# Later places for the sums of squared attention outputs and for the query transposes in a hand-ordered attention

## The chip, the cores and the metric

The kernel runs on one core of a Trainium2 chip. The metric is the device time of one execution in microseconds (us), the median of several runs. The engines are named as in the profile: PE is TensorE, DVE is VectorE, ACT is ScalarE, POOL is GpSimd and SP is SyncE, which here only issues DMAs.

## The reference

The reference is a backbone of two layers over 512 latent tokens and 256 context tokens of width 1024. Layer 0 mixes tokens by differential attention, layer 1 by a short gated convolution, and each ends with a SwiGLU FFN; adaLN shifts, scales and gates come from a conditioning vector. The part that matters here is the attention of layer 0, with 8 heads of two maps of 64 and a value width of 128:

```python
def _diff_attend(q, k, v, lam):
    s = jnp.einsum("bqmhd,bkmhd->bmhqk", q, k) * (HEAD_DIM ** -0.5)
    p = jax.nn.softmax(s, axis=-1)
    a = (p[:, 0] - lam * p[:, 1]).astype(v.dtype)
    return jnp.einsum("bhqk,bkhd->bqhd", a, v)

q = rmsnorm(q, q_norm); k = rmsnorm(k, k_norm)        # per head and map
q_l, k_l = apply_rope(q_l, cos, sin), apply_rope(k_l, cos, sin)
o = rmsnorm(o, subln) * (1.0 - lam_init)              # per token and head
y = o.reshape(bsz, -1, DIFF_V_WIDTH) @ w_o
```

Queries are the 512 latent tokens, keys and values all 768. The last norm needs, for each token and head, the sum of the squares of the attention's 128 outputs.

## The kernel before, in words

Activations lie with features on partitions. Every float32 product is made of three products of fp32r parts (high by high, high by low, low by high), so each operand is split into two parts: ACT casts the high part, DVE or POOL subtracts the low one.

The attention is a pipeline over the heads. While head h is attended, the projections of head h+1 are made token tile by token tile (`pq_{h+1}_t`, 24 products of 384 columns, or of 256 for the context tiles 4 and 5), and during head 7 the output projection of the first six heads (`pw_n`). A head takes 24 positions, each with a quarter of such a tile. What else is issued stands in an agenda that `events` (L635 to L644) fills from tables of positions (L15 to L38): `trans_k` (tiles `tk_h_g`: transposes of two token tiles of keys; ACT casts KH, DVE subtracts KL), `trans_q` (tile `tq_h`; ACT casts Q0 and Q1, DVE subtracts), `scores` (tiles `s_h_t_m`, the row maximum `l` on DVE, the exponentials `e` on ACT), `trans_a` (tiles `ta_h_t_g`: transposes of the attention weights; ACT casts ATh, DVE subtracts ATl) and `pv` (tile `pv_h_half`: attention weights times values for half of the queries, 18 products of 256 columns). All these PSUM tiles except the scores and projections come from one pool, `ptr`, with tag "tr" and 2 buffers: a tile's first write waits until the tile two before it has been read by ACT and DVE.

At the end of `pv` ACT squares the outputs into `osq` (L539) and copies them to `oT` (L540), DVE takes the minimum with a bound (L541), TensorE sums the squares with two small float32 products into a tile `po_h_half` (L542 to L545) and DVE adds that tile to `stat` (L546). In head 6 `o_rstd` (L553) turns the sums of the first six heads into `or_0`; SP stores it to `rst_dram` (L562) and loads it back, broadcast to all partitions, into `obc0` to `obc5` (L567); DVE scales the outputs `oT` with it (L568); they are split into the parts `oh` and `ol` for `pw_n`. The tiles `h_n` (L624) hold the residual stream and lie over `aTh_n`, an operand of the projections. `ada` (L191) are DVE products of streamed adaLN weights that fill the attention, with a raw buffer that the `obc` and the output weights `raw_wo` share.

In the start TensorE is pinned to the order of the program; from L366 on it is not, and a list scheduler orders the instructions of every engine from the order of issue and its own estimates. TensorE, DVE, ACT, POOL and SP each run their queue in that order.

Of the kernel before, what the change touches and what calls it, by code (L numbers as in the profile page):

```python
# [7 lines left out]
F32 = mybir.dt.float32  # L8
# [6 lines left out]
# The order of issue in the attention. A head takes 24 positions, each with a quarter of the projections of  # L15
# one token tile of the next head (head 7: of one feature tile of the output projection); what else is issued,
# and at which position of its head, is listed here.
#   scores 0, scores 1, transpose 0, scores 2, transpose 1, scores 3, transpose 2, P V of tiles 0-1, transpose 3, P V of tiles 2-3
AT = (6, 9, 11, 12, 16, 16, 20, 19, 22, 28)
AT_OF = {0: (10, 14, 16, 16, 20, 21, 22, 21, 26, 27), 1: (7, 8, 11, 12, 12, 16, 21, 19, 23, 28),  # L20
         6: (8, 9, 14, 6, 16, 17, 23, 18, 24, 28), 7: (5, 7, 10, 9, 13, 8, 16, 15, 16, 23)}
#   transposes of k tiles 2-3, q, k tiles 4-5 (head 0: k tiles 0-1, 2-3, q, k tiles 4-5)
TK = (2, 0, 4)
TK_OF = {0: (9, 9, 8, 10), 1: (0, 2, 4), 7: (3, 0, 3)}
#   transposes of k tiles 0-1 of the next head
TK_NEXT = 16
TK_NEXT_OF = {0: 12, 6: 15}
#   the weights of the head after the next, by feature tiles
W_AT = (16, 19, 22, 23, 23, 24, 26, 27)
W_AT_OF = {0: (11, 11, 15, 22, 22, 22, 25, 26)}  # L30
#   positions from the squares of a token tile to its rotation
LAG = 1
LAG_OF = {1: 0}
#   head 6: scale of the first six heads' outputs, its products, their exact parts
# [3 lines left out]
# halves of adaLN tiles per token tile of each head, per pair of gate and up tiles, per down tile  # L38
ADA_HEAD = (0, 2, 1, 1, 1, 1, 1, 1)
ADA_GATE, ADA_DOWN = 3, 3  # L40
# tile of the output projection before which the weights of the last two heads are staged
W67_AT = 6
# token tiles whose squares the activation engine also sums
ACC_TILES = (0, 1, 2, 3, 4)
# second parts of staged weights: 0 on the vector engine, 1 on the GpSimd engine
# [6 lines left out]
# the first head's projections: at which feature tile the second head's weights are staged, how many tiles the  # L52
# context lags behind the latent tokens, where its statistics and their broadcast come
# [5 lines left out]
# pieces of the second half of the tokens after which the next norm's statistics and its products come  # L59
TURN = {8: (4, 7), 2: (1, 3)}  # L60
# feature tiles whose squares GpSimd sums for the norm after the attention
POOL_SUMS = (1, 3, 5)
P = 128
# [3 lines left out]
KT = 8  # L67
# [10 lines left out]
# columns of the packed parameters  # L78
# [9 lines left out]
class InOrder:  # L88
    """an engine; while pin is set its instructions are issued in program order"""
# [16 lines left out]
def kernel(  # L106
# [43 lines left out]
    mods = const.tile([P, 2, 6, KT], F32, name="mods")      # sh1 sc1 g1 sh2 sc2 g2  # L150
    part = const.tile([P, 2, 2, 6, KT], F32, name="part")   # halves of the dot products
    mod0 = const.tile([P, 2, 2, KT], F32, name="mod0")      # layer 0, latent and context: sh1 sc1
    Gc = const.tile([P, 5, KT], F32, name="Gc")             # norm gains times (1 + scale)
# [9 lines left out]
    # staging of the attention weights and the attention output: right stack  # L163
# [22 lines left out]
    def ada_half(i, half, pool, tag, bufs):  # L186
        """one half of the dot products of a tile of 128 columns of ada_w with silu(c)"""
# [15 lines left out]
    # =====================================================================  # L203
    # layer 0: modulated input, differential attention
    # =====================================================================
# [23 lines left out]
    # the tensor engine's clock rises while the first loads are under way  # L229
# [25 lines left out]
    def bcast(dgs, bc):  # L255
        """bc[t][:, q] = rstd of token q of tile t, the same on all partitions"""
        for dg, o in zip(dgs, bc):
            te.matmul(out=o, lhsT=ones, rhs=dg, start=True, stop=True)
# [827 lines left out]
```

## Time and profile before

| | |
|---|---|
| median of 3 runs | 1342.76 us (1341.63 to 1345.31) |
| profiled execution, span from first to last instruction | 1343.2 us |
| mean granted TensorE clock | 0.991 |
| PE busy | 1309.2 us (97%) |
| DVE busy | 809.6 us (60%) |
| ACT busy | 503.9 us (38%) |
| POOL busy | 184.9 us (14%) |
| attention (heads 0 to 7) | from about 66 to 399 us, some 40 us a head |

The shares of the whole span say little on the attention: DVE's 60% is an average over the attention and the FFNs, where it has little to do. The windows of a stretch show what each engine does in it; the list of waits shows for which producer TensorE sat idle; the timelines show single instructions, with the idle time before each and what ended it in brackets.

### The profile page before, as it was taken

The page shows a single profiled execution, that of the slowest core. Times are in us where ns is not written, and L with a number is a line of the kernel's source. Part 1 is how long each engine was busy: PE and PEld are TensorE (multiplying, and loading weights), DVE is VectorE, ACT ScalarE, POOL GpSimd, SP SyncE. Part 2 cuts the span into 40 slices and gives each one's busy share as a digit, 9 for nine tenths or more (in the row PEclk, how much of TensorE's full clock was granted, in tenths as well). Part 3 has the DMA queues.
Part 4 walks back from the last instruction along what each step waited for, and adds up shares of the span by engine and source line. Part 5 has one row for each costly group of instructions (what it writes and reads, how often), then busy time and mean ns, then how long its engine had stood idle before and what let it go on. Part 6 is the DMA issues. An engine that isn't in the chain of part 4 may idle for free.

```text
span 1343.2 us, 18899 instructions
## 1 busy us (share of the span) xinstructions
PE 1309.2 (97%) x7021; PEld 1130.8 (84%) x7021; DVE 809.6 (60%) x1598; ACT 503.9 (38%) x1125; POOL 184.9 (14%) x239
## 2 busy tenths in 40 slices
PE   8999999999999999899999999999999999999999
PEld 7889988998789888688888898888898888888887
DVE  5889888988968666665653366444664333333331
ACT  4677666776655321122221333222342212222120
POOL 0544444543302000000000020000100000000000
PEclk9999999999998999899999999999999999999999
DMA  9413333214333756677642333313323223322231
GB/s 350 160 41 112 94 95 90 71 59 146 106 118 103 224 197 196 198 241 224 203 134 67 110 109 109 97 55 96 118 72 121 81 72 109 125 94 85 70 105 40
DMA packets 72284, 164.59 MB, mean 123 GB/s; under 512 B 7784, under 2 KB 23424, under 8 KB 71168
## 3 DMA queue, kind: packets, MB, share of 16 engines
q1 hardware_dynamic: 72192, 163.38, 38.6%
q8 instruction: 55, 0.90, 0.3%
q14 instruction: 37, 0.30, 0.1%
HBM read 161.24 MB, written 2.11 MB: 122 GB/s over the span
## 4 chain that ended last, share of the span: by engine, by line
PE 74%; DVE 10%; DMA 8%; issue 3%; POOL 2%; ACT 2%; SPq 0%; POOLq 0%; DVEq 0%; ACTq 0%
PE pg L98 25%; PE pd L98 18%; PE pi L98 8%; PE pq L98 7%; DMA ada<-in_adaR_dram 6%; PE py L98 3%; PE s L98 3%; PE pw L98 3%; DVE ada L191 2%; PE pf_in L98 2%; PE pf_gu L98 2%; PE pv L98 1%; DMA xk<-in_xT_dram 1%; POOL st L432 1%; DMA raw_w<-in_wqkv_dram 1%
## 5 line engine op out<-in xcount | busy, mean ns | idle before, releaser
L727 ACT CAST sh_gu<-sr_gu 128x1024 fp32r<-128x1024 f32 x88 | 92.3, 1052 | 276.1 <-PE pg L98 147.9
L191 DVE SCALAR_TENSOR_TENSOR ada<-ada,scrow 128x512 f32<-128x512 f32 x160 | 110.6, 702 | 85.5 <-DMA ada<-in_adaR_dram 85.1
L728 DVE TENSOR_TENSOR sl_gu<-sr_gu,sh_gu 128x1024 fp32r<-128x1024 f32 x85 | 105.8, 1247 | 72.4 <-ACT sh_gu L727 65.3
L98 PE MATMUL pg<-xl_n0b,sh_gu 128*128 128x512 f32 x320 | 124.6, 389 | 0.0
L98 PE MATMUL pg<-xh_n0b,sh_gu 128*128 128x512 f32 x320 | 124.6, 389 | 0.0
L98 PE MATMUL pg<-xh_n1b,sh_gu 128*128 128x512 f32 x320 | 124.6, 389 | 0.0
L98 PE MATMUL pg<-xl_n1b,sh_gu 128*128 128x512 f32 x320 | 124.5, 389 | 0.0
L98 PE MATMUL pg<-xh_n1b,sl_gu 128*128 128x512 f32 x320 | 124.5, 389 | 0.0
L98 PE MATMUL pg<-xh_n0b,sl_gu 128*128 128x512 f32 x320 | 124.5, 389 | 0.0
L98 PE MATMUL pq<-hi_w,aTl 128*128 128x384 f32 (+1 forms) x336 | 108.5, 323 | 0.0
L98 PE MATMUL pq<-hi_w,aTh 128*128 128x384 f32 x224 | 77.3, 345 | 2.5 <-DVE qn L443 2.5
L839 DVE TENSOR_TENSOR sl<-sl,pg 128x512 f32<-128x512 f32 x40 | 27.4, 686 | 85.7 <-PE pg L98 85.7
L98 PE MATMUL pq<-lo_w,aTh 128*128 128x384 f32 x224 | 76.3, 341 | 0.0
L98 PEld LDWEIGHTS pg<-xh_n1b,sh_gu 128*128 128x128 f32 x320 | 60.1, 188 | 12.5
L98 PEld LDWEIGHTS pg<-xl_n0b,sh_gu 128*128 128x128 f32 x320 | 60.1, 188 | 12.5
L98 PEld LDWEIGHTS pg<-xh_n1b,sl_gu 128*128 128x128 f32 x320 | 60.1, 188 | 12.5
L98 PEld LDWEIGHTS pg<-xh_n0b,sh_gu 128*128 128x128 f32 x320 | 60.1, 188 | 12.5
L98 PEld LDWEIGHTS pg<-xl_n1b,sh_gu 128*128 128x128 f32 x320 | 60.1, 188 | 12.3
L98 PEld LDWEIGHTS pg<-xh_n0b,sl_gu 128*128 128x128 f32 x320 | 60.1, 188 | 12.3
L504 ACT ACTIVATE e<-s,l 128x768 f32<-128x768 f32 x64 | 58.0, 908 | 29.5 <-DVE l L502 18.4
L502 DVE TENSOR_REDUCE l<-s 128x1 f32<-128x768 f32 x64 | 60.0, 949 | 8.3 <-PE s L98 7.8
L98 PEld LDWEIGHTS pq<-hi_w,aTl 128*128 128x128 f32 x336 | 63.9, 190 | 0.0
(390 smaller groups left out, 3366.7 us busy)
## 6 DMA issues: line engine op xcount, KB each, us to landing
sr_gu<-in_wgu_dram SPq DMA_DIRECT2D x88, 512.0 KB, 3.9
ada<-in_adaR_dram SPq DMA_DIRECT2D x160, 256.0 KB, 3.2
raw_w<-in_wqkv_dram SPq DMA_DIRECT2D x64, 192.0 KB, 2.6
sr_in<-in_win_dram SPq DMA_DIRECT2D x24, 512.0 KB, 3.5
ad<-in_ada_dram SPq DMA_DIRECT2D x8, 1024.0 KB, 8.8
raw_wo<-in_wo_dram SPq DMA_DIRECT2D x16, 192.0 KB, 2.8
xk<-in_xT_dram SPq DMA_DIRECT2D x8, 256.0 KB, 5.3
h<-in_xT_dram SPq DMA_DIRECT2D x8, 256.0 KB, 6.1
```

The lines of the kernel that those rows point to most:

```text
L98: ins = f(*args, **kw)
L191: ve.scalar_tensor_tensor(out=raw, in0=raw, scalar=1.0, in1=scrow[:, half * 512:(half + 1) * 512], op0=ALU.mult, op1=ALU.mult, accum_out=p ...
L432: nc.gpsimd.tensor_tensor(out=st[:, 4:4 + ns], in0=st[:, 0:ns], in1=nhalf[:, 0:ns], op=ALU.pow)
L502: ve.tensor_reduce(out=l[:, m:m + 1], in_=s[:, :, 0:384], axis=AX.XY, op=ALU.max, negate=True)
L504: ae.activation(out=em.rearrange("p (a b) -> p a b", a=2), in_=s[:, :, 0:384], func=AF.Exp, bias=l[:, m:m + 1], scale=1.0, accum_out=l[:, ...
L727: ae.copy(out=hi[:, :ncols], in_=raw[:, :ncols])
L728: lo_eng.tensor_tensor(out=lo[:, :ncols], in0=raw[:, :ncols], in1=fp(hi)[:, :ncols], op=ALU.subtract)
L839: ve.tensor_tensor(out=t[:, s], in0=t[:, s], in1=ps_u, op=ALU.mult)
```

## The change

The last part of `pv` becomes a piece of its own, `po`, with its own positions (`PO`): at positions 22 and 35 of a head in most heads, that is, the second half is issued 11 positions into the next head. Before, they came at the positions of `pv`, 19 and 28. The table `TK` moves the query transposes of heads 2 to 6 from position 0 to 2, and those of head 7 from 0 to 3, behind the transposes of key tiles 2 and 3. Comments were taken out as well, which shifts line numbers by some lines.

```diff
+PO = (22, 35)
+PO_OF = {0: (26, 31), 1: (23, 35), 5: (22, 32), 6: (24, 36), 7: (18, 25)}
-TK = (2, 0, 4)
-TK_OF = {0: (9, 9, 8, 10), 1: (0, 2, 4), 7: (3, 0, 3)}
+TK = (2, 2, 4)
+TK_OF = {0: (9, 9, 8, 10), 1: (0, 2, 4), 7: (3, 3, 3)}
...
         ae.activation(out=osq, in_=p, func=AF.Square)
         ae.copy(out=oT[h][:, sl], in_=p)
         ve.tensor_scalar(out=osq, in0=osq, scalar1=BIG, scalar2=None, op0=ALU.min)
+        o.osq[half] = osq
+
+    def po(o, half):
+        h, osq = o.h, o.osq[half]
         p2 = ptr.tile([P, P], F32, name=f"po_{h}_{half}", tag="tr")
         r = slice(64 * half, 64 * half + 64)
         for g in range(2):
...
-        e += zip(AT_OF.get(h, AT), todo)
+        at = AT_OF.get(h, AT)
+        e += zip(at, todo)
+        e += zip(PO_OF.get(h, PO), (lambda: po(o, 0), lambda: po(o, 1)))
```

Since the scheduler starts from another order of issue, the queues of all engines change. Names below end in a running number of the tile.

**TensorE, from head 3 to head 4** (the projections `pq_5` run between). The start of `pq_5_0`, before and then with the change:

```order
L98 MATMUL pq_5_0_2992<-hi_w5_0_2794,aTh0_97 128x384
L98 MATMUL pq_5_0_2992<-lo_w5_0_2795,aTh0_97 128x384
L98 MATMUL pq_5_0_2992<-hi_w5_0_2794,aTl0_113 128x384
L98 MATMUL tq_4_2983<-cst_sb_62,qrp_4_2544 128x128 x4
L98 MATMUL pq_5_0_2992<-hi_w5_1_2861,aTh1_98 128x384
L98 MATMUL pq_5_0_2992<-lo_w5_1_2862,aTh1_98 128x384
```

```order
L101 MATMUL pq_5_0_2983<-hi_w5_0_2794,aTh0_97 128x384
L101 MATMUL pq_5_0_2983<-lo_w5_0_2795,aTh0_97 128x384
L101 MATMUL po_3_0_2922<-osq_3_0_2851,cst_sb_62 32x128 x2
L101 MATMUL pq_5_0_2983<-hi_w5_0_2794,aTl0_113 128x384
L101 MATMUL pq_5_0_2983<-hi_w5_1_2857,aTh1_98 128x384
L101 MATMUL pq_5_0_2983<-lo_w5_1_2858,aTh1_98 128x384
```

`po_3_0` stands now where `tq_4` stood, one product earlier; `tq_4` comes nine products later, right behind `tk_4_1`. The end of `pv_3_1`, before and then with the change:

```order
L98 MATMUL pv_3_1_3049<-ATh_3_1_2882,vl_3_1886 128x256
L98 MATMUL pq_5_1_3093<-hi_w5_0_2794,aTh0_97 128x384
L98 MATMUL pq_5_1_3093<-lo_w5_0_2795,aTh0_97 128x384
L98 MATMUL pq_5_1_3093<-hi_w5_0_2794,aTl0_113 128x384
L98 MATMUL pq_5_1_3093<-hi_w5_1_2861,aTh1_98 128x384
L98 MATMUL pq_5_1_3093<-lo_w5_1_2862,aTh1_98 128x384
L98 MATMUL pq_5_1_3093<-hi_w5_1_2861,aTl1_114 128x384
L98 MATMUL pq_5_1_3093<-hi_w5_2_2928,aTh2_99 128x384
L98 MATMUL po_3_1_3072<-osq_3_1_3068,cst_sb_62 32x128 x2
L98 MATMUL tk_4_2_3076<-cst_sb_62,krp_4_2_2898 128x128 x4
L98 MATMUL pq_5_1_3093<-lo_w5_2_2929,aTh2_99 128x384
```

```order
L101 MATMUL pv_3_1_3049<-ATl_3_1_2879,vh_3_1885 128x256
L101 MATMUL pv_3_1_3049<-ATh_3_1_2878,vl_3_1886 128x256
L101 MATMUL tk_4_2_3072<-cst_sb_62,krp_4_2_2894 128x128 x4
L101 MATMUL pq_5_1_3089<-hi_w5_0_2794,aTh0_97 128x384
L101 MATMUL pq_5_1_3089<-lo_w5_0_2795,aTh0_97 128x384
L101 MATMUL pq_5_1_3089<-hi_w5_0_2794,aTl0_113 128x384
```

`po_3_1` has left (it now stands in `pq_5_2`, in front of `ta_4_0_0`), and `tk_4_2` follows `pv_3_1` at once.

**VectorE, the same stretch**, before and then with the change (from Q0 of head 4 to the min on `osq_3_1`):

```order
L477 TENSOR_TENSOR Q0_4_2425<-tq_4_2983,Q0_4_2425 64x512
L443 TENSOR_TENSOR qn_4_5_2979<-pq_4_5_2901,st_4_5_2958 128x128
L181 TENSOR_TENSOR lo_w5_7_3027<-raw_w5_7_3024,hi_w5_7_3026 128x384
L477 TENSOR_TENSOR Q1_4_2426<-tq_4_2983,Q1_4_2426 64x512
L488 TENSOR_TENSOR KL_4_2428<-tk_4_1_3011,KH_4_2427 128x2x256
L191 SCALAR_TENSOR_TENSOR ada_12_0_3046,part_69<-ada_12_0_3046,scrow_72 128x512
L191 SCALAR_TENSOR_TENSOR ada_12_1_3149,part_69<-ada_12_1_3149,scrow_72 128x512
L191 SCALAR_TENSOR_TENSOR ada_13_0_3230,part_69<-ada_13_0_3230,scrow_72 128x512
L191 SCALAR_TENSOR_TENSOR ada_13_1_3298,part_69<-ada_13_1_3298,scrow_72 128x512
L433 TENSOR_TENSOR vl_5_2972<-pq_5_0_2992,vh_5_2971 128x128
L443 TENSOR_TENSOR qn_5_0_3083<-pq_5_0_2992,st_5_0_3037 128x256
L541 TENSOR_SCALAR osq_3_1_3068<-osq_3_1_3068 128x256
```

```order
L184 TENSOR_TENSOR lo_w5_7_3027<-raw_w5_7_3024,hi_w5_7_3026 128x384
L194 SCALAR_TENSOR_TENSOR ada_12_0_3046,part_69<-ada_12_0_3046,scrow_72 128x512
L194 SCALAR_TENSOR_TENSOR ada_12_1_3145,part_69<-ada_12_1_3145,scrow_72 128x512
L492 TENSOR_TENSOR KL_4_2428<-tk_4_1_3002,KH_4_2427 128x2x256
L481 TENSOR_TENSOR Q0_4_2425<-tq_4_3009,Q0_4_2425 64x512
L194 SCALAR_TENSOR_TENSOR ada_13_0_3230,part_69<-ada_13_0_3230,scrow_72 128x512
L194 SCALAR_TENSOR_TENSOR ada_13_1_3298,part_69<-ada_13_1_3298,scrow_72 128x512
L481 TENSOR_TENSOR Q1_4_2426<-tq_4_3009,Q1_4_2426 64x512
L194 SCALAR_TENSOR_TENSOR ada_14_0_3417,part_69<-ada_14_0_3417,scrow_72 128x512
L184 TENSOR_TENSOR lo_w6_1_3400<-raw_w6_1_3397,hi_w6_1_3399 128x384
L437 TENSOR_TENSOR vl_5_2972<-pq_5_0_2983,vh_5_2971 128x128
L545 TENSOR_SCALAR osq_3_1_3068<-osq_3_1_3068 128x256
```

KL and the two Q now stand behind two `ada` products, the second Q behind four.

**Head 6, SP's queue**, before and then with the change:

```order
L562 DMA rst_dram_727<-or_0_4326 6x128 x4
L567 DMA obc0_4335<-rst_dram_727 128x4x128
L567 DMA obc1_4338<-rst_dram_727 128x4x128
L567 DMA obc3_4341<-rst_dram_727 128x4x128
L567 DMA obc2_4380<-rst_dram_727 128x4x128
L567 DMA obc4_4396<-rst_dram_727 128x4x128
L190 DMA ada_19_1_4415<-in_adaR_dram 128x512
L624 DMA h0_4670<-in_xT_dram 128x512
L624 DMA h1_4776<-in_xT_dram 128x512
L624 DMA h2_4869<-in_xT_dram 128x512
L567 DMA obc5_4499<-rst_dram_727 128x4x128
```

```order
L633 DMA h0_4670<-in_xT_dram 128x512
L571 DMA rst_dram_727<-or_0_4326 6x128 x4
L633 DMA h1_4772<-in_xT_dram 128x512
L633 DMA h2_4865<-in_xT_dram 128x512
L633 DMA h3_4941<-in_xT_dram 128x512
L576 DMA obc0_4335<-rst_dram_727 128x4x128
L576 DMA obc1_4338<-rst_dram_727 128x4x128
L576 DMA obc3_4341<-rst_dram_727 128x4x128
L576 DMA obc2_4380<-rst_dram_727 128x4x128
L576 DMA obc4_4396<-rst_dram_727 128x4x128
L193 DMA ada_19_1_4415<-in_adaR_dram 128x512
L576 DMA obc5_4495<-rst_dram_727 128x4x128
```

`h0` now stands ahead of the four stores and `h1` to `h3` ahead of the loads `obc`. **VectorE with the change**, where these loads are used; before, the products `oT0`, `oT1` and `oT3` stood among other work 15 to 20 rows ahead of `ATl_6_0`:

```order
L577 SCALAR_TENSOR_TENSOR oT0_81<-oT0_81,misc_65,obc0_4335 128x512
L577 SCALAR_TENSOR_TENSOR oT1_82<-oT1_82,misc_65,obc1_4338 128x512
L577 SCALAR_TENSOR_TENSOR oT3_84<-oT3_84,misc_65,obc3_4341 128x512
L437 TENSOR_TENSOR vl_7_4058<-pq_7_3_4353,vh_7_4057 128x128
L577 SCALAR_TENSOR_TENSOR oT2_83<-oT2_83,misc_65,obc2_4380 128x512
L577 SCALAR_TENSOR_TENSOR oT4_85<-oT4_85,misc_65,obc4_4396 128x512
L531 TENSOR_TENSOR ATl_6_0_4367<-ta_6_1_0_4418,ATh_6_0_4366 128x3x128
L194 SCALAR_TENSOR_TENSOR ada_19_1_4415,part_69<-ada_19_1_4415,scrow_72 128x512
L531 TENSOR_TENSOR ATl_6_0_4367<-ta_6_1_1_4424,ATh_6_0_4366 128x3x128
L447 TENSOR_TENSOR qn_7_3_4430<-pq_7_3_4353,st_7_3_4406 128x256
```

The five products `oT` now stand in a row, but for one `vl`, ahead of the `ATl_6_0` that is made from `ta_6_1`. **ACT in head 6**, before and then with the change:

```order
L573 CAST oh3_4634<-oT4_85 128x512
L180 CAST hi_wo0_0_4617<-raw_wo0_0_4615 128x384
L504 ACTIVATE e0_6_3_4452,l_6_3_4445<-s_6_3_0_4446,l_6_3_4445 128x768
L539 ACTIVATE osq_6_0_4491<-pv_6_0_4472 128x256
L540 COPY oT6_87<-pv_6_0_4472 128x256
L504 ACTIVATE e1_6_3_4460,l_6_3_4445<-s_6_3_1_4454,l_6_3_4445 128x768
```

```order
L582 CAST oh3_4625<-oT4_85 128x512
L543 ACTIVATE osq_6_0_4491<-pv_6_0_4472 128x256
L508 ACTIVATE e0_6_3_4452,l_6_3_4445<-s_6_3_0_4446,l_6_3_4445 128x768
L544 COPY oT6_87<-pv_6_0_4472 128x256
L183 CAST hi_wo0_0_4608<-raw_wo0_0_4606 128x384
L508 ACTIVATE e1_6_3_4460,l_6_3_4445<-s_6_3_1_4454,l_6_3_4445 128x768
```

The square `osq_6_0` and the exponentials `e0_6_3` now stand ahead of the cast `hi_wo0_0`.

## Rows read from the trace of the kernel before

**Rows 1.** Windows, core 0: us from and to, length, busy us (instructions), PEclk, DMA share, GB/s.
```profile
180.00:230.00 50.00, 47.03 (x320) 44.65 (x319) 44.05 (x101) 31.76 (x104) 24.39 (x35) 1.00 0.33 103
```
**Rows 2.** Waits of TensorE: releaser, us in total, times, longest us.
```profile
PE po L98 <- DVE osq L541: 7.8, 6, 3.2
...
PE tq L98 <- DVE ATl L527: 2.0, 4, 0.5
...
PE ta L98 <- DVE ATl L527: 0.7, 4, 0.2
```
**Rows 3.** Timeline of TensorE, end of head 3: start us, duration, instruction [idle before].
```profile
218.55 0.66 PE L98 MATMUL tq<-cst_sb,qrp 128*128 128x128 f32 x4 [0.53 <-DVE ATl L527]
...
223.13 0.28 PE L98 MATMUL pv<-ATh,vh 128*128 128x256 f32 x1
223.25 0.28 PE L98 MATMUL pv<-ATl,vh 128*128 128x256 f32 x1
...
227.81 0.41 PE L98 MATMUL po<-osq,cst_sb 128*32 128x128 f32 x4 [1.15 <-DVE osq L541]
...
229.52 0.34 PE L98 MATMUL s<-KH,Q 128*128 128x384 f32 x1
```
**Rows 4.** Timeline of VectorE, the same stretch.
```profile
221.84 0.69 DVE L477 TENSOR_TENSOR Q<-tq,Q 64x512 fp32r<-64x512 f32 x1
222.57 0.69 DVE L488 TENSOR_TENSOR KL<-tk,KH 128x512 fp32r<-128x512 f32 x1
223.17 0.68 DVE L191 SCALAR_TENSOR_TENSOR ada<-ada,scrow 128x512 f32<-128x512 f32 x1
...
226.93 0.74 DVE L541 TENSOR_SCALAR osq<-osq 128x256 f32<-128x256 f32 x1
...
230.98 1.81 DVE L502 TENSOR_REDUCE l<-s 128x1 f32<-128x768 f32 x2
```
**Rows 5.** Timeline of TensorE, head 6.
```profile
330.73 0.39 PE L98 MATMUL pv<-ATh,vh 128*128 128x256 f32 x1 [0.53 <-DVE ATl L527]
...
337.86 0.41 PE L98 MATMUL po<-osq,cst_sb 128*32 128x128 f32 x4 [3.19 <-DVE osq L541]
...
341.28 0.42 PE L98 MATMUL pq<-hi_w,aCh 128*128 128x256 f32 x1
341.49 0.40 PE L98 MATMUL pq<-lo_w,aCh 128*128 128x256 f32 x1
```
**Rows 6.** Timeline of ACT, head 6.
```profile
335.58 0.51 ACT L180 CAST hi_wo<-raw_wo 128x384 fp32r<-128x384 f32 x1 [3.87 <-DMA raw_wo<-in_wo_dram]
...
336.88 0.37 ACT L539 ACTIVATE osq<-pv 128x256 f32<-128x256 f32 x1
```
**Rows 7.** Windows in head 6, columns as in rows 1.
```profile
320.00:324.00 4.00, 4.00 (x26) 3.68 (x25) 4.00 (x7) 2.30 (x6) 3.23 (x4) 1.00 1.03 296
...
336.00:340.00 4.00, 2.14 (x13) 1.97 (x14) 2.72 (x9) 3.92 (x10) 2.14 (x3) 0.79 0.27 73
```
**Rows 8.** Timeline of SP in head 6: start of the first issue, us, issues in a row.
```profile
312.81 1.35 SPq L562 DMA_DIRECT2D rst_dram<-or  x4
315.20 3.12 SPq L567 DMA_DIRECT2D obc<-rst_dram  x5
...
321.15 1.38 SPq L624 DMA_DIRECT2D h<-in_xT_dram  x3
```
**Rows 9.** The tile `obc`: us from issue to landing of its six loads.
```profile
DMA to landing us min/median/max: 4.6/6.1/6.4
```
**Rows 10.** Timeline of VectorE in head 6.
```profile
328.66 0.73 DVE L568 SCALAR_TENSOR_TENSOR oT<-oT,misc,obc 128x512 f32<-128x512 f32 x1
...
330.13 1.01 DVE L527 TENSOR_TENSOR ATl<-ta,ATh 128x384 fp32r<-128x384 f32 x2
```
**Rows 11.** Timelines of VectorE and TensorE at the end of the attention.
```profile
393.09 0.28 DVE L557 SCALAR_TENSOR_TENSOR or<-stat,or 128x128 f32<-128x128 f32 x1
...
396.18 0.39 PE L98 MATMUL pw<-oh,lo_wo 128*128 128x512 f32 x1
396.40 0.83 PE L98 MATMUL pob<-or,cst_sb 128*128 128x128 f32 x6
```

More of the change, by code (lines that the diff above doesn't have):

```diff
@@ L409, in new_head @@
         o.AT = {}
+        o.osq = {}
         o.a = {}
```

## The prediction

> **What bounds the kernel now.** I read the windows of the attention first. In a stretch that holds one head and a quarter TensorE is busy for 47 of 50 us and VectorE for 44 [rows 1]: TensorE sets the time, and VectorE, which makes almost everything that TensorE's transposes and products wait for, has only 6 us in 50 to spare. An order of issue can therefore win no more than TensorE's holes, and what it takes off one wait on VectorE may come back as the next.
>
> The list of TensorE's waits names the holes [rows 2]. The sums of the squared outputs (`po`, which wait for the min on `osq`) cost 7.8 us in 6 waits, the longest 3.2. The query transposes (`tq`) cost 2.0 us in 4, the transposes `ta` 0.7 in 4. These 9.8 us of `po` and `tq` are what the change touches.
>
> The timeline of TensorE at the end of head 3 shows the small kind [rows 3]: `pv_3_1` starts at 223.13, `po_3_1` comes at 227.81 after 1.15 us idle, head 4's scores start at 229.52. VectorE shows why [rows 4]: the min on `osq` starts only at 226.93, behind KL (222.57) and the `ada` products (from 223.17, 0.62 us apart). The six waits less the longest are 7.8 - 3.2 = 4.6 us, in the second halves of heads 1 to 5, 0.9 each.
>
> The large kind is `po_6_0` [rows 5]: at 337.86 after 3.19 us. ACT's rows give the cause [rows 6]: the cast `hi_wo` waits 3.87 us for its DMA, and the square of `osq` stands behind it in ACT's queue (336.88). The granted clock is 0.79 in the stretch after this stall, against 1.00 before [rows 7]: part of it ran at the lower of the two levels, 1.2 instead of 2.4 GHz. Products of 256 columns are 0.21 us apart there (341.28, 341.49) [rows 5], against 0.12 at full clock (223.13, 223.25) [rows 3]. From the end of `po` (338.27) to 341.70 that is 3.4 us for what would take 3.4 x 0.12/0.21 = 2.0: some 1.5 us lost besides the wait.
>
> **The change, part by part.** It adds and removes no arithmetic; it moves 16 `po` groups and the 8 query transposes, and since the queues are scheduled anew after the start, the DVE, ACT, POOL and SP orders with them.
>
> *Heads 1 to 5, `po_h_0` and `tq`.* `po_3_0` now stands where `tq_4` stood, in the first rows of `pq_5_0` and one row earlier. TensorE waited there for VectorE's ATl, 0.53 us at `tq` (218.55) [rows 3]. It will do so again, since ATl's place behind VectorE's work is not earlier: of the 2.0 us I take none as won. Ends: -2.0 if all goes, and 0. `ta_h_3_0` is reached sooner by the `po` that has left (0.41 us by the record at 227.81 [rows 3]) while its ATl is not, so its wait grows by about as much; nothing is won there either.
>
> *Heads 1 to 5, `po_h_1`.* The 0.9 us wait disappears, since the group now comes a token tile later. But it held two buffers apart. The pool "tr" has two. `pv_3_1` now takes the one of `tk_4_1`, which VectorE's KL frees; in VectorE's new order KL stands behind two `ada`. From the end of `lo_w` (before KL and Q, 221.84 [rows 4]): 221.84 + 2 x 0.62 = 223.1, KL 0.69, so `pv` starts at about 223.8 where it started at 223.13: 0.7 us of waiting. `tk_4_2` follows `pv` at once and takes the buffer of `tq`, freed by the second Q: after KL (223.8) come Q 0.69, two `ada` 1.24 and Q 0.69, that is 226.4, while `pv` ends at 223.8 + 18 x 0.12 = 226.0: another 0.4. So 1.1 us is waited in the place of 1.15. The group itself (0.41) is paid a little later. Head 4's scores then start at about 229.3 in place of 229.52, and VectorE reaches its first reduction at 230.98 [rows 4] as before, because its work up to there is the same. I take 0 per head; bounds -0.9 (no new wait) and +0.9 (the new waits add to those left), so 0 over five heads, from -4.6 to +4.6.
>
> *Head 6, `po_6_0`.* On ACT the square of `osq_6_0` now precedes `hi_wo`, and `po_6_0` stands behind ten products of `pw_0`. The wait of 3.19 and the 1.5 of slow clock go: -4.7.
>
> *Head 6, SP's queue.* What is late next is the scale of the first six heads. Before, SP issued the four `rst_dram` stores, then five `obc` loads from 315.20, and the `h` loads from 321.15 [rows 8]. Now `h1` to `h3` stand ahead of `obc0`, and `h_k` overwrites `aTh_k`, so they wait for the products of `pq_7_3` that read it; the first issue of `h` at 321.15 is a bound near which these are free. Three `h` issues (1.38) make `obc0` about 322 to 323, 7 us later. Five take 3.1 and land 4.6 to 6.4 us after issue [rows 9], with the DMA engines at 1.03 of their time in 320 to 324 already [rows 7]: the fifth lands at about 331 to 332. VectorE's new order has all five products `oT` (0.73 us each and more, the last at 328.66 before) ahead of the ATl that `pv_6_0` waits for, which ran at 330.13 [rows 10]. So ATl comes at 332.5 to 334 and `pv_6_0`, which started at 330.73 [rows 5], about 2 to 4 us later; with the clock falling again perhaps 1.5 more. I take +3.2. The cover that would make it nothing is other work in VectorE's and TensorE's queues ahead of these, which ran at 320 to 324 beside `oT` before and shifts forward. Bounds: 0 and +7.2, so head 6 as a whole -4.7 to +2.5; likeliest -1.5.
>
> *Head 7.* `po_7_1` moves behind four products of 512 columns, 0.22 us each (396.18 to 396.40 [rows 11]), 0.9 us. The chain that hangs on it ends at 393.09 + 0.28 = 393.4, and TensorE reaches `pob` at 396.40 [rows 11]: 3.0 us of cover, so 0. From there on nothing changes.
>
> **Sum.** 0 + 0 - 1.5 + 0 = -1.5 us against the profiled execution's 1343.2, whose span I take as its time: 1341.7. The median of the three runs, 1342.76, is 0.4 lower, so I predict 1341.3. About 0.3% (4.0 us) is what a measurement of this kernel can tell from no change; the forecast's own range is 1337.5 to 1345.
>
> **The rivals.**
> *Faster, the holes really close.* If KL and Q are ready when `pv` and `tk_h_2` come, the 4.6 us are won; if `obc` lands in time, 4.7 in head 6. Together 9.3, about 1333.5. For it: VectorE has 6 us in 50 idle [rows 1], so a shuffle can pay; against it: KL and Q now stand behind more `ada` than before. A half of it (say -5) is already past the 0.3%. Chance 0.34.
>
> *Slower, the `obc` loads hold VectorE.* Place: head 6, SP's queue behind `h3`; price: ATl, and with it `pv_6_0` and the scores' reductions behind it, 7 us late plus 1.5 of slow clock, less the 4.7 won, +2.5 to +4; it decides from the point where `pv_6_0` waits over 4.7 us. With 0.3 us left over per head in the other heads it gives about 1347. For it: the DMA share of 1.03; against it: TensorE has other rows to do ahead of `pv_6_0`. Chance 0.20.
>
> *Slower, transposes in a row.* `tk_h_1` and `tq_h` now stand side by side, eight transposes. If such a run let the clock fall each time, it would cost what the stall of `po_6_0` cost, 1.5 us, in five heads: +7.5, about 1350. The rows speak against it: the stretch 180 to 230 holds many transposes at a granted clock of 1.00 [rows 1]. Chance 0.02. The Trainium skill (TensorE: Matmul & The Clock Gate, Part 4: PE-mode transpose) says that transposes do not count as busy time for the clock in the way that other products do; no row of this trace shows a fall by them, so by that rule alone I give no more.
>
> **How the numbers follow.** The forecast, within 0.3%, has 0.44. Faster by over 0.3% is the first rival, 0.34; slower the two others, 0.22. The range 1334 to 1347.5 takes in the forecast's own range, the second rival's price and all but the full price of the first; what is left out is that full price and the transposes, under 2 in 10.
>
> **What would show it.** Right: `po` gone from the list of waits, or below 3 us and waiting for ATl instead of `osq`; new waits of `pv` and `tk` for KL and Q of 0.4 to 0.7 us in heads 2 to 5; `obc0` issued after 321; a wait at `pv_6_0` of 2 to 4 us in the place of 3.19 at `po_6_0`. Wrong: no wait at `pv` and `tk` (faster), `obc0` issued before 318 (faster by 3), or a granted clock below 0.9 somewhere between 80 and 320 (slower).

## The result, and the profile after

The changed kernel takes 1358.47 us, the median of 6 runs (1355.13 to 1364.61); six runs of the kernel before gave 1342.71 (1341.29 to 1345.31). The ratio is 1.0117, interval [1.0099, 1.0136]: about 16 us slower, outside the predicted range.

The profiled execution of the change is its fastest run, 1355.13 us, with a span of 1353.2; so a run's own time is some 2 us above its span, which the prediction took as equal. By the same 2 us the profiled execution of before took some 1345.2, the upper end of its six runs; so the two profiles, whose spans differ by 10.0 us (1343.2 and 1353.2), show less than the 16 us of the medians. Their windows (start, attention, the rest; columns as in [rows 1]) show where. Before:

```profile
66.00:400.00 334.00, 318.35 (x2060) 294.30 (x2059) 292.49 (x660) 221.42 (x679) 140.15 (x197) 0.99 0.31 94
400.00:1340.00 940.00, 930.69 (x4518) 784.09 (x4517) 468.42 (x819) 245.09 (x339) 25.09 (x16) 0.99 0.40 123
```

After:

```profile
66.00:420.00 354.00, 326.38 (x2070) 296.85 (x2069) 294.81 (x661) 220.78 (x680) 140.83 (x198) 0.99 0.29 89
420.00:1350.00 930.00, 924.47 (x4513) 778.10 (x4511) 467.49 (x818) 244.40 (x339) 25.12 (x16) 1.00 0.40 125
```

In these windows of the attention TensorE is idle for 354.00 - 326.38 = 27.6 us, before for 334.00 - 318.35 = 15.7, with the same mean clock. Below, "the attention" is the time from the first score product `s_0_0_0` to `pob6`: before, 75.41 to 396.40 [rows 11], 320.99 us; after, by these two rows of TensorE's timeline, 415.66 - 77.04 = 338.62, **17.6 us longer**.

```profile
77.04 0.44 PE L101 MATMUL s<-KH,Q 128*128 128x384 f32 x1
...
415.66 0.61 PE L101 MATMUL pob<-or,cst_sb 128*128 128x128 f32 x4
```

Between these two products TensorE does the same number of products in both kernels. It is idle for 24.5 us against 12.4, which makes 12.1 of the 17.6; the other 5.5 are products that are busy for longer, and no run shows what each of them costs.

Another 1.6 us is the start, whose code is the same (in the profiles of all runs it ends between 74.8 and 79.4 us). The lead of the kernel before, 17.0 us at its 540, shrinks to 9.9 behind the first `pd` of the FFN: there before's TensorE had this wait, `gh` being behind `ada` products in VectorE's queue, and the first products after it took 0.79 us where the change's take 0.49 (granted clock 0.50 from 554 to 558; in the change 1.00 from 566 to 570):

```profile
PE pd L98 <- DVE gh L840: 5.7, 1, 5.7
```

The change has 1.1 us there:

```profile
PE pd L101 <- DVE gh L851: 1.1, 1, 1.1
```

This wait lay between 1.1 and 5.7 us in the profiles of all runs and does not follow the attention: the change in heads 0 to 5 alone, below, has an attention 16.7 us longer and 5.0 us here, the one in heads 6 and 7 alone 0.6 us shorter and 2.3. The medians don't show the 7 us either (16 us against 17.6 in the attention). So versions are compared by medians and by the attention alone.

By the first score product of token tile 0 of each head (`s_h_0_0`; in head 6 those of tile 2 come before it), the change falls behind by 2.45 us at head 1, 3.58, 5.44, 8.80, 13.06 and 14.96 at head 6, and 19.26 at `pob6`. So heads 1 to 5 cost 12.5, heads 6 and 7 4.3, head 0 0.8. (In the change six products more stand behind `s_6_0_0` than before; at equal numbers of products heads 6 and 7 cost 3.2, those ahead of them 14.5.) TensorE's waits, 66 to 420 us, against [rows 2]:

```profile
PE ta L101 <- DVE ATl L531: 4.1, 5, 1.0
PE pv L101 <- DVE ATl L531: 3.7, 1, 3.7
PE pv L101 <- DVE KL L492: 3.1, 4, 0.8
PE tk L101 <- DVE ATl L531: 2.9, 5, 0.7
...
PE s L101 <- ACT e L508: 2.3, 4, 1.3
PE s L101 <- DVE KL L492: 1.7, 3, 0.9
PE ta L101 <- DVE e L514: 1.5, 1, 1.5
PE tk L101 <- DVE Q L481: 1.5, 3, 0.5
PE ta L101 <- DVE stat L555: 1.4, 3, 0.6
PE po L101 <- DVE ATl L531: 0.8, 2, 0.6
...
PE po L101 <- DVE osq L545: 0.4, 1, 0.4
```

`po` for `osq` fell from 7.8 to 0.4, as the change says. In its place stand nine kinds of wait of 1.4 us and more. Six are for the PSUM tag "tr": `pv`, `tk` and `ta` wait for KL, Q, ATl or `stat`, VectorE's last readers of an older tile. Three are of another sort: scores for ACT's `e`, which has to read an older score tile, and scores for KL and `ta` for VectorE's `e`, which are their operands. Yet VectorE idles more, not less: the two windows 180 to 230 [rows 1] and 230 to 280 show 41.24 and 41.53 us of work in 50 (third column of busy times), before 44.05 and 44.33. The second of these before, then both after:

```profile
230.00:280.00 50.00, 49.08 (x325) 47.22 (x324) 44.33 (x102) 34.41 (x117) 21.54 (x32) 1.00 0.26 78
...
180.00:230.00 50.00, 45.21 (x301) 41.34 (x300) 41.24 (x92) 30.51 (x98) 23.16 (x34) 1.00 0.26 82
230.00:280.00 50.00, 44.63 (x296) 41.06 (x295) 41.53 (x95) 29.65 (x102) 21.94 (x30) 1.00 0.28 86
```

What VectorE waits for, after, 66 to 420 us:

```profile
DVE qn L447 <- POOL st L436: 14.9, 19, 1.0
DVE e L514 <- ACT e L513: 9.3, 13, 1.2
...
DVE ada L194 <- DMA ada<-in_adaR_dram: 4.3, 5, 2.1
```

The third line is the lead. VectorE's timeline at the start of head 4, the stretch of [rows 4], shows the longest of these:

```profile
236.28 0.55 DVE L184 TENSOR_TENSOR lo_w<-raw_w,hi_w 128x384 fp32r<-128x384 f32 x1
...
238.11 0.67 DVE L492 TENSOR_TENSOR KL<-tk,KH 128x512 fp32r<-128x512 f32 x1
...
241.74 0.69 DVE L194 SCALAR_TENSOR_TENSOR ada<-ada,scrow 128x512 f32<-128x512 f32 x1 [2.09 <-DMA ada<-in_adaR_dram]
242.35 0.08 DVE L194 DVE_READ_ACCUMULATOR ada<-ada,scrow 128x1 f32 x1
242.35 1.82 DVE L506 TENSOR_REDUCE l<-s 128x1 f32<-128x768 f32 x2
```

SP issued that load only at 238.15, after `lo_w` (236.28) had freed the raw buffer that it goes into:

```profile
238.15 0.93 SPq L193 DMA_DIRECT2D ada<-in_adaR_dram  x1
```

The buffer was free at 236.83, with the end of `lo_w`; until 237.73 SP stood at the weight load ahead of it in its queue, whose buffer POOL's `lo_w` had still to read. This is SP's longest wait from 230 to 240 us:

```profile
SPq L180 <- POOL lo_w L184: 2.4, 1, 2.4
```

TensorE's timeline has the price:

```profile
238.32 0.34 PE L101 MATMUL s<-KH,Q 128*128 128x384 f32 x1
...
244.39 0.44 PE L101 MATMUL s<-KH,Q 128*128 128x384 f32 x1 [1.27 <-ACT e L508]
```

The maxima `l_4_0` run 4.0 us after their scores began (238.32 to 242.35); before it was 1.5 (229.52 [rows 3] to 230.98 [rows 4]). The next scores then wait 1.27 us for the exponentials that free their PSUM. Before, this second half of the `ada` stood behind the maxima, so its load had time:

```profile
233.12 0.69 DVE L191 SCALAR_TENSOR_TENSOR ada<-ada,scrow 128x512 f32<-128x512 f32 x1 [0.33 <-DMA ada<-in_adaR_dram]
```

In head 3 of the change this product has come ahead of the maxima too, in heads 1, 2 and 5 it has not. From a head's first scores to its first maxima it took, in heads 1 to 5, 1.88, 1.32, 1.45, 1.46 and 1.45 us before and 2.59, 2.37, 3.68, 4.04 and 2.28 after: all are later, but only in heads 3 and 4 does VectorE's timeline have this product, and its wait for the DMA (0.93 and 2.09 us), ahead of the maxima.

### The profile page after: what moved, and what is told of

It is laid out like the page before. It is cut to its first block, busy times and chain, and to the rows that moved or that the text cites. A ratio compares the mean times of both kernels' runs of the same rounds, so it can differ in the third digit from the quotient of the medians.

```text
span 1353.2 us, 18899 instructions
## 1 busy us (share of the span) xinstructions
PE 1311.2 (97%) x7021; PEld 1127.0 (83%) x7021; DVE 810.4 (60%) x1598; ACT 502.7 (37%) x1125; POOL 185.6 (14%) x239
## 4 chain that ended last, share of the span: by engine, by line
PE 71%; DVE 10%; DMA 8%; ACT 5%; issue 3%; POOL 2%; SPq 0%; POOLq 0%; DVEq 0%; ACTq 0%
PE pg L101 25%; PE pd L101 18%; PE pi L101 8%; DMA ada<-in_adaR_dram 6%; PE pf_gu L101 3%; PE py L101 3%; PE pq L101 3%; PE pw L101 2%; DVE ada L194 2%; PE pv L101 2%; PE pf_in L101 2%; POOL st L436 1%; PE q L101 1%; PE s L101 1%; ACT e L513 1%
## 5 line engine op out<-in xcount | busy, mean ns | idle before, releaser
L101 PEld LDWEIGHTS pg<-xl_n0b,sh_gu 128*128 128x128 f32 x320 | 60.1, 188 | 12.5
L101 PEld LDWEIGHTS pg<-xl_n1b,sh_gu 128*128 128x128 f32 x320 | 60.1, 188 | 12.5
L101 PEld LDWEIGHTS pg<-xh_n0b,sh_gu 128*128 128x128 f32 x320 | 60.1, 188 | 12.4
L101 PEld LDWEIGHTS pg<-xh_n0b,sl_gu 128*128 128x128 f32 x320 | 60.1, 188 | 12.4
L750 DVE SCALAR_TENSOR_TENSOR h<-pd,mods,h 128x512 f32<-128x512 f32 (+1 forms) x35 | 24.6, 704 | 63.3 <-PE pd L101 63.2
```

The lines of the kernel that those rows point to most:

```text
L101: ins = f(*args, **kw)
L750: ve.scalar_tensor_tensor(out=h, in0=ps, scalar=gcol[:, n:n + 1], in1=h, op0=ALU.mult, op1=ALU.add)
```

## The experiments

In all of them the diff is against the changed kernel unless said otherwise; with the tables put back to the old positions the order is that of before, as far as the runs show it (with heads 6 and 7 alone changed, TensorE's products stand in the order of before up to 298 us). "Loss" is the median against the kernel before on the same chip, "attention" the difference to 320.99 us in the profile.

**Which moves cost: positions put back in parts.** Two theories stood: that the sums `po`, moved between other "tr" tiles, hold up the ring of two buffers; and that the new VectorE order with `ada` ahead of the maxima does it, whichever move brought it about.

Only the sums are moved, the query transposes are where they were:

```diff
-TK = (2, 2, 4)
-TK_OF = {0: (9, 9, 8, 10), 1: (0, 2, 4), 7: (3, 3, 3)}
+TK = (2, 0, 4)
+TK_OF = {0: (9, 9, 8, 10), 1: (0, 2, 4), 7: (3, 0, 3)}
```

> Only the later places of po (table PO); the query transposes stay where they were (table TK of before). Theory A, the ring of two 'tr' buffers: without po between them, transposes and P V products take buffers that VectorE frees late (waits of tk and ta for ATl, of ta for stat), so po carries most of the loss: 8 to 13 us slower than before, waits of tk and ta for ATl as with the whole change (7 us), but pv waiting for KL under 1 us. Theory B, an ada product ahead of the score maxima in VectorE's queue: its second half stands there in this order too, so scores wait for e as with the whole change (2.3 us or more). If instead the query transposes are the cause: within 3 us of before.

1358.46 against 1344.14 us, ratio 1.0104 [1.0087, 1.0121]: loss 14; attention +15.6.

Only the query transposes are moved:

```diff
-PO = (22, 35)
-PO_OF = {0: (26, 31), 1: (23, 35), 5: (22, 32), 6: (24, 36), 7: (18, 25)}
+PO = (19, 28)
+PO_OF = {0: (21, 27), 1: (19, 28), 6: (18, 28), 7: (15, 23)}
```

> Only the later query transposes (table TK); po right behind its pv as before. Theory A: the waits for osq stay (about 7.8 us), pv waits for KL and tk for Q (4 us in all are added): 2 to 5 us slower than before. Theory B: in this order two halves of ada stand ahead of the score maxima, so the loss is as large as with po alone, 6 us or more, with scores waiting for e. If po is the whole cause: within 2 us of before.

1356.85 us, 1.0095 [1.0075, 1.0115]: loss 13; attention +12.4. With no sum moved, sums in between can't be the whole cause. Each move alone costs nearly what both cost together, so they share a cause at least in part. With the transposes alone the largest waits of TensorE are

```profile
PE po L101 <- DVE osq L545: 10.7, 6, 3.7
PE s L101 <- ACT e L508: 5.8, 7, 1.3
...
PE pv L101 <- DVE KL L492: 1.5, 4, 0.8
```

and of VectorE

```profile
DVE ada L194 <- DMA ada<-in_adaR_dram: 8.2, 4, 2.6
```

The change in heads 0 to 5 alone, then in heads 6 and 7 alone:

```diff
+PO_OF = {0: (26, 31), 1: (23, 35), 5: (22, 32), 6: (18, 28), 7: (15, 23)}
+TK_OF = {0: (9, 9, 8, 10), 1: (0, 2, 4), 6: (2, 0, 4), 7: (3, 0, 3)}
```

> The change in heads 0 to 5, heads 6 and 7 at the positions of before. If each head pays its own 3 us, and head 6 pays for the obc loads behind h1 to h3 (an order that this kernel still has): within 3 us of the whole change, 13 to 17 slower than before, pv_6_0 waiting 3 us or more. If the loss of head 6 comes from head 6's own positions: 10 to 12 slower than before, no long wait at pv_6_0.

```diff
+PO = (19, 28)
+PO_OF = {0: (21, 27), 1: (19, 28), 6: (24, 36), 7: (18, 25)}
+TK = (2, 0, 4)
+TK_OF = {0: (9, 9, 8, 10), 1: (0, 2, 4), 6: (2, 2, 4), 7: (3, 3, 3)}
```

> The change in heads 6 and 7 alone; SP's order around the obc loads is that of before. If the loss is paid per head and by the late obc loads: no loss here, and the stall of 3.2 us at po_6_0 gone, 1 to 5 us faster than before. If head 6's own positions cost: 2 to 5 us slower.

Heads 0 to 5: 1360.13 us, 1.0112 [1.0087, 1.0137], the whole loss; attention +16.7, with the wait of `pv_6_0` (3.6 us) still in it. Heads 6 and 7: 1343.47, 0.9993 [0.9982, 1.0005], no change; attention -0.6. So the new positions of head 6 bring nothing and the wait at `pv_6_0` comes from the heads before.

**The `ada` product put behind the maxima.** In heads 2 to 6 the last half of `ada` of each head is tied behind the second maximum of the first token tile. By VectorE's timelines this changes its place where it had come ahead of the maxima: in heads 3 and 4 of the whole change, in heads 3 to 5 with the sums alone and in heads 2 to 5 with the transposes alone. In the whole change a later maximum moves a few places with it in these heads, two rows move on TensorE and none on SP.

```diff
+        with tc.issue_after(behind) if behind is not None else ExitStack():
+            ve.scalar_tensor_tensor(out=raw, in0=raw, scalar=1.0, in1=scrow[:, half * 512:(half + 1) * 512], op0=ALU.mult, op1=ALU.mult,
...
+            o.lmax[t, m] = ve.tensor_reduce(out=l[:, m:m + 1], in_=s[:, :, 0:384], axis=AX.XY, op=ALU.max, negate=True).ins
...
+                ada_some(ADA_HEAD[h], stA, "raw", RAW_BUFS, o.lmax[0, 1] if 2 <= h <= 6 and slot == 5 else None)
```

With the whole change:

> The whole change, and in heads 2 to 6 the second ada half that VectorE's queue had ahead of the head's first score maxima (ada_8_1, ada_11_1, ada_14_1, ada_17_1) is queued behind them; TensorE's order moves by two rows, SP's not at all. Theory B, that this product waits for a load that SP can only just have issued, and holds up the maxima, the exponentials and the next scores: its DMA wait ahead of the maxima goes (2.1 us at ada_14_1), scores stop waiting for e, and 5 to 9 of the 16 us come back. Theory A, the ring of 'tr' buffers alone: within 2 us of the whole change.

With the query transposes alone (the second kernel above plus this edit):

> The later query transposes alone, and the same ada halves behind the maxima. Theory B: this part's loss lies all between the start of a head's scores and its third tile, so nearly all of its 12 us comes back: within 4 us of before. Theory A: no change against the query transposes alone, 12 us slower than before.

With the sums alone (the first plus this edit):

> The later po alone, and the same ada halves behind the maxima. Theory B: 5 to 9 of its 14 us come back; what is left, waits of tk and ta for ATl and of pv for Q, is the part of Theory A, 5 to 9 us against before. Theory A alone: no change against po alone, 14 us slower than before.

Query transposes: 1347.4 against 1344.36, 1.0025 [1.0011, 1.004], so 9 of the 13 us are back; attention +3.3 in place of +12.4, and TensorE's list keeps the `po` line and loses the one of `s` for `e`:

```profile
PE po L101 <- DVE osq L547: 10.5, 6, 3.5
...
PE pv L101 <- DVE KL L494: 1.5, 4, 0.8
```

That shows the mechanism for this half: the first maxima of heads 2 to 5 come 1.25 to 1.85 us after their scores, where they came 3.46 to 4.06 after them. In the whole change the edit brings heads 3 and 4 back from 3.68 and 4.04 to 1.23 and 1.24 us and gives back 5.7 us of the attention (+11.9), by the medians 4 (1356.5 against 1344.36, 1.01 [1.0069, 1.0132], an interval that overlaps the change's own); with the sums alone 4.4 of the attention (+11.2; 1355.4, 1.0076 [1.0046, 1.0105]). Most of the rest there must have another cause.

**KL and Q ahead of the other `ada`.** With the edit above in place, the other five `ada` products of heads 2 to 6, four of which stood ahead of the second Q, are tied behind the last subtraction of Q; some rows of TensorE and ACT move with them:

```diff
+                ada_some(ADA_HEAD[h], stA, "raw", RAW_BUFS, (o.lmax[0, 1] if slot == 5 else o.q1) if 2 <= h <= 6 else None)
```

> The whole change, with VectorE's queue mended in heads 2 to 6 at two places: the second ada half behind the head's first score maxima, and KL and both Q ahead of the four ada that stood in front of them; SP's order is that of the change. If the 'tr' buffers that VectorE frees late are what the rest is (Theory A): the waits of pv for KL (4.0 us with their latency) and of tk for Q (2.0) go, and 4 to 7 us come back against the kernel with the first mend alone: 5 to 8 us slower than before. If those waits only hide others, the waits of ta and tk for ATl grow instead and it stays 10 to 13 slower than before.

1349.97 against 1343.26 us, 1.0043 [1.0029, 1.0057]: by the medians another 5 back, 9 of the change's 16 with both edits. `pv` for KL and `tk` for Q are gone from the list. Up to `s_6_0_0` the attention is now 5.1 us longer (13.3 in the change, 8.8 with `ada` behind alone). The whole is +10.5, only 1.5 better than with `ada` behind alone, because the wait at `pv_6_0` grew; here alone the median and the attention of the one profile are nearly 4 us apart:

```profile
PE pv L101 <- DVE ATl L533: 5.1, 1, 5.1
```

**Head 6: why `obc` is late.** In the profile of the change SP's timeline reads

```profile
335.28 0.33 SPq L633 DMA_DIRECT2D h<-in_xT_dram  x1
335.70 1.36 SPq L571 DMA_DIRECT2D rst_dram<-or  x4
337.16 1.30 SPq L633 DMA_DIRECT2D h<-in_xT_dram  x3
338.68 4.89 SPq L576 DMA_DIRECT2D obc<-rst_dram  x5
```

and VectorE's

```profile
345.64 1.60 DVE L577 SCALAR_TENSOR_TENSOR oT<-oT,misc,obc 128x512 f32<-128x512 f32 x2 [0.75 <-DMA obc<-rst_dram]
...
349.19 0.75 DVE L577 SCALAR_TENSOR_TENSOR oT<-oT,misc,obc 128x512 f32<-128x512 f32 x1 [1.08 <-DMA obc<-rst_dram]
349.86 0.55 DVE L531 TENSOR_TENSOR ATl<-ta,ATh 128x384 fp32r<-128x384 f32 x1
```

so that TensorE stood at `pv_6_0`:

```profile
350.46 0.58 PE L101 MATMUL pv<-ATh,vh 128*128 128x256 f32 x1 [3.67 <-DVE ATl L531]
```

`obc0` is issued 10.5 us after `s_6_0_0` (328.23); before, 1.9 (313.28 to 315.20 [rows 8]). Two theories: the `h` loads that now stand ahead of it in SP's queue (the prediction's), or `po_5_1`, the last sum that `or_0` needs, which `PO_OF[5]` puts at position 32, 4 later than before (21.0 us later in the trace, 306.89 to 327.89, where `s_6_0_0` is 15.0 later). The first is undone by queueing the `h` loads behind the fifth `obc`, with `ada` behind as above:

```diff
+        with tc.issue_after(obc_dma[4]):
+            nc.sync.dma_start(out=t, in_=xT[:, n, 0:SEQ])
```

> As the first of these, and in head 6 SP's loads h0 to h3 are queued behind the obc loads as before the change. If the late obc loads make the 3.7 us wait of pv_6_0: obc0 is issued 6 us or more earlier against the scores of head 6, the wait of pv_6_0 for ATl is under 1 us, and 2 to 4 us more come back, less what the cast of the output weights, which then stands ahead of osq_6_0 again, takes. If not: that wait stays.

1359.1 against 1344.36, 1.0107 [1.0077, 1.0136]: nothing won. `obc0` came 9.3 us after `s_6_0_0` (10.4 without this edit), and a wait of 2.2 us at `pv_6_0` was left (2.4 without). SP's order explains 1.1 us of the lateness and not the rest. The second, again with `ada` behind:

```diff
-PO_OF = {0: (26, 31), 1: (23, 35), 5: (22, 32), 6: (24, 36), 7: (18, 25)}
+PO_OF = {0: (26, 31), 1: (23, 35), 5: (22, 28), 6: (24, 36), 7: (18, 25)}
```

> The whole change with the first mend (ada half behind the maxima), and the last sums of head 5, po_5_1, at position 28 instead of 32. If head 6 loses because po_5_1 itself comes late, so that or_0 and the obc loads start late: obc0 is issued within 5 us of the start of the scores of head 6's first tile, where it took 10.4 with the change and 1.9 before; the wait of pv_6_0 for ATl is under 1.5 us and 2 to 4 us come back against the kernel with the first mend alone. If the late loads only hide other waits of head 6: no difference within 2 us.

1353.39 against 1343.26, 1.008 [1.0057, 1.0103]. SP's timeline:

```profile
326.87 1.34 SPq L573 DMA_DIRECT2D rst_dram<-or  x4
329.25 3.11 SPq L578 DMA_DIRECT2D obc<-rst_dram  x5
```

`obc0` is again 1.9 us behind `s_6_0_0` (327.34), and the wait at `pv_6_0` is 0.5 as before. From `s_6_0_0` to `pob6` the kernel is now 0.6 us shorter than before; without the edit it was 3.1 longer. Some 1.1 of these 3.7 us are the six products that stand ahead of `s_6_0_0` again, so 2.5 are won. Of them 1.5 are paid ahead of it, 0.8 as the early `po_5_1` waits for its `osq` again, so the attention stands at +10.9 in place of +11.9. By the medians the two can't be told apart. So `po_5_1` is shown to set when `obc0` is issued and whether `pv_6_0` waits; that it is worth 2.5 us rests on one profile each.

**First sums or second sums.** With the transposes at their old places and `ada` behind, only the second, then only the first sum of each head is moved:

```diff
+PO = (19, 35)
+PO_OF = {0: (21, 31), 1: (19, 35), 5: (19, 32), 6: (18, 36), 7: (15, 25)}
```

> Only the second sums of each head (po_h_1) later, first sums and query transposes as before, the ada half behind the maxima. If the second sums carry the loss (pv takes the buffer of the query transposes, freed by Q behind ada; ta_h_0_1 waits for stat; head 6's obc loads are late): the attention is 7 to 10 us longer than before, waits of pv for Q 3 us or more. If the first sums carry it: under 4 us longer.

```diff
+PO = (22, 28)
+PO_OF = {0: (26, 27), 1: (23, 28), 5: (22, 28), 6: (24, 28), 7: (18, 23)}
```

> Only the first sums (po_h_0) later, the rest as before, the ada half behind the maxima. If the waits of ta and tk for ATl come from the first sums: these stay (3 us or more above before) and the attention is 3 to 6 us longer. If not: within 2 us of before, and the gain of 2 to 5 us at po_6_0 may show.

Second sums: 1346.95 against 1343.68, 1.0018 [1.0007, 1.003]; attention +4.1, of which 1.5 up to `s_6_0_0` and the rest behind it, with a wait of 3.0 at `pv_6_0`. First sums: 1349.85, 1.0047 [1.0029, 1.0066]; attention +7.0, 5.6 of it up to `s_6_0_0` and 3.7 in heads 0 and 1. I had expected the opposite weight: the prediction had argued over the second sum at length, and the first costs more.

**All mends together.** KL and Q first, the last half of `ada` behind the maxima, and `po_5_1` at 28:

> The whole change with all three mends: ada half behind the maxima, KL and Q ahead of ada, po_5_1 at position 28. If the three causes add: the 10.5 us that the attention has with the first two mends fall to 4 to 6, and the kernel is within 5 us of before. If head 6's loss has another cause: 9 us or more longer.

1350.9 against 1343.68, 1.0052 [1.0035, 1.0068]; attention +5.8, so from +17.6 the three edits take 11.8 away. By the medians the loss is 7 us, no less than without the move of `po_5_1` (1.0043), and over the 5 that was expected. What is left on TensorE, in the main:

```profile
PE ta L101 <- DVE ATl L533: 4.7, 6, 1.0
PE s L101 <- DVE KL L494: 3.0, 4, 1.2
...
PE tk L101 <- DVE ATl L533: 2.2, 3, 0.8
```

`ta` and `tk` again wait for VectorE to read an older "tr" tile, and the sums are now one of the tiles in between. That the first sum's place makes them is argued from this list and the run above, not shown by an edit of its own.

**The same holes, closed on VectorE.** The prediction's aim can be had without moving the sums: before, `osq`'s min stood behind `qn`, which waits for POOL (0.65 us in head 3), as VectorE's timeline ahead of the min of [rows 4] shows:

```profile
226.59 0.42 DVE L443 TENSOR_TENSOR qn<-pq,st 128x256 f32<-128x256 f32 x1 [0.65 <-POOL st L432]
```

In the kernel before, `qn` of the head after next is queued behind the min; TensorE's sum then stands two products earlier:

```diff
+        omin[h, half] = ve.tensor_scalar(out=osq, in0=osq, scalar1=BIG, scalar2=None, op0=ALU.min).ins
...
+        with tc.issue_after(omin[h - 2, 1]) if t == 0 and (h - 2, 1) in omin else ExitStack():
+            ve.tensor_tensor(out=qn[:, 4 - ns:4], in0=ps[:, n0:256].rearrange("p (s d) -> p s d", d=HD),
```

> The kernel before with nothing of the change, but VectorE's min on osq of each head's second half ahead of the query and key product qn that waits for GpSimd. If the waits of po in heads 2 to 5 (0.9 us each) are this place in VectorE's queue: they fall by 0.4 to 0.7 us each, and the attention is 1 to 3 us shorter, 0 to 3 us faster than before. If VectorE sets the pace there anyway: no difference within 1 us.

The same edit on the kernel with heads 6 and 7 alone changed:

> The same, with the change in heads 6 and 7 alone (which took 0.6 us off the attention in its profile). If both add: the attention is 2 to 4 us shorter than before, and the kernel 1 to 4 us faster. If not: within 1 us of before.

1340.49 against 1343.26, 0.9985 [0.997, 0.9999], attention -1.9; with the new heads 6 and 7 1341.27, 0.9986 [0.9973, 1.0], attention -1.7. The gain is small, its intervals end at 0.9999 and 1.0; the two do not add. Last, the edit on the kernel before together with the one thing of the change that frees `po_6_0`, ACT's cast `hi_wo0_0` queued behind the square of `osq_6_0`:

```diff
+        with tc.issue_after(osq6[0]) if tagn == "wo0_0" else ExitStack():
+            ae.copy(out=hi[:, :ncols], in_=raw[:, :ncols])
```

> The kernel before with the min on osq ahead of qn, and ACT's cast of the first output weights behind the square of osq_6_0; TensorE's, VectorE's and SP's orders are those of the first mend alone. If the stall of po_6_0 behind that cast costs what the prediction took (3.2 us and 1.5 of slow clock): that wait goes, and the attention is 3 to 5 us shorter than with the first mend alone, 4 to 7 us faster than before. If the time is lost again at the first output products, which need that cast: under 1.5 us.

1339.68 against 1343.68 us, **0.9967 [0.9955, 0.9979]**: 4 us faster than the kernel before, and the fastest here; attention -4.6. Against the first edit alone the intervals overlap; that the second adds something is seen in the attention and in the waits. TensorE's `po` line shows both edits: 7.8 us in 6 waits before [rows 2], 5.2 in 3 with the first alone, and now

```profile
PE po L101 <- DVE osq L553: 2.3, 2, 1.2
```

## Why the prediction was wrong

**The step that failed** is "I take 0 per head" for `po_h_1`, with its reason that VectorE reaches its first reduction "because its work up to there is the same". Measured, heads 1 to 5 cost 12.5 us, 2.5 per head, against bounds of -0.9 to +0.9. The work is the same, its order is not. In heads 3 and 4 an `ada` half had come in front of the maxima, whose load waits for `lo_w`, just ahead in the same queue, to free its buffer, and for the load ahead of it on SP; these two heads cost the most, 3.36 and 4.26 us. The prediction counted what stands ahead of KL and Q by its durations and never asked whether each of these instructions would be ready; the row `[2.09 <-DMA ada]` is what that misses. With that half tied behind the maxima the transposes alone lose 3 us in place of 13, and the whole change is 8.8 us late at `s_6_0_0` in place of 13.3.

The second reason for the zero, that the new waits take the place of the one removed, was half right. The waits of `pv` for KL (up to 0.8) and `tk` for Q (up to 0.5) have the sizes that were worked out (0.7 and 0.4), and the holes at `po` did go (7.8 us to 0.4). But they were not all that came in exchange: `ta` and `tk` now wait for ATl, scores for KL. Setting KL and Q first as well leaves 5.1 us at `s_6_0_0`, and by the medians 9 of the change's 16 us are back with TensorE's tables as in the change. So more than half of the loss is shown to come from VectorE's order, as far as the few rows that move on TensorE with each edit leave it alone. What makes the last 5 to 7 us stays open: that the ring of "tr" buffers passes the delay on from tile to tile is read from the list of waits, not shown by an edit of its own. Head 0, whose sums move too, had no term; it cost 0.8 us.

**`po_h_0` and `tq`, 0.** Wrong too: the wait did not stay where it was. `tq` no longer waits for ATl, but `tk` (2.9 us) and `ta` (4.1, before 0.7) do. With the first sums alone moved, the attention is 7.0 us longer, more than half of it in heads 0 and 1; the bound had been 0 from above.

**Head 6, `po_6_0`, -4.7.** The wait of 3.19 us vanished. Its size in the time is smaller: freeing it alone takes the attention from -1.9 to -4.6, 2.8 us by one profile each. In the change heads 6 and 7 lose all the same.

**Head 6, `obc`, +3.2.** The sign and size held: 3.7 us at `pv_6_0`, 2 to 4 had been given, and the granted clock fell as it had at [rows 7], to 0.57:

```profile
350.00:354.00 4.00, 3.54 (x17) 3.54 (x18) 4.00 (x10) 0.59 (x1) 0.00 (x0) 0.57 0.88 286
```

The cause did not, so the size was right by luck. The `h` loads ahead of it were worth 1.1 us (10.4 to 9.3), and `or_0` itself was late, through `po_5_1`: the prediction followed the buffers and SP's queue behind `or_0`, not the sum in front of it.

**Head 7, 0** held as far as it can be told: heads 6 and 7 moved alone left the time as it was.

**The signs.** All that the prediction named for being right came: `po` below 3 us, `pv` and `tk` waiting for KL and Q, `obc0` after 321 (338.68), 3.67 us at `pv_6_0`. None of its signs for being wrong did. They looked where waits were expected, and none at the first maxima or at `ta`, where the time went.

**The rivals.** The slower one named the right place in head 6, but its point of decision (over 4.7 us at `pv_6_0`) was not reached, and the loss lay elsewhere. The one of transposes in a row falls: `tk_4_1` and `tq_4` stand side by side at 228.97 and 229.40, and the granted clock is 1.00 in both windows from 180 to 280. So the rule of the Trainium skill that was weighed there (TensorE: Matmul & The Clock Gate, Part 4: PE-mode transpose) explains nothing of the loss. The faster rival's holes can close, with the sums where they were and the orders of VectorE and ACT mended: 4 us, of the 9.3 it hoped for.

## What to carry to other kernels

When an order of issue changes, look in the new queue for each instruction fed by a DMA, find what frees its buffer and which loads are issued ahead of its own, and ask whether these stand shortly ahead; whatever is behind it waits for the load. A tile moved in time also moves in its ring of buffers: write the ring's new sequence down and check each reader, for a wait taken off one user can come back at the next. Where an engine has 6 us in 50 to spare, move the one late instruction within its queue before moving the work that waits for it.

## What was not expected

Two moves that cost 14 and 13 us alone cost 16 together. The `ada` half ahead of the maxima is a part that they share: putting it behind gives back 4.4 and 9.1 us of the attention with one move alone and 5.7 with both. Why the rest does not add up was not shown. A stage that the change does not touch made the two profiles differ by 7 us less than the attention did, by a wait that varies from profile to profile: one pair of profiles would have hidden over a third of the loss. And VectorE, the engine that TensorE waits for, was idle for 3 us more in 50: it was not short of time, but stood waiting for POOL (14.9 us against 5.8), ACT and DMA, in head 4 with maxima behind it whose scores were done.
